# Attention values multiplied with tokens on partitions, and the convolution's first tap on GpSimd

## The chip, the core and the metric

The kernel runs on one core of one Trainium2 chip. The metric is the device time of one execution in microseconds; lower is better. The engines of the core are TensorE (PE: matmuls, with its weight loads as PEld), VectorE (DVE), ScalarE (ACT), GpSimd (POOL) and SyncE (SP, which here issues the loads of weights). Matmuls write to PSUM, a small memory of banks that DVE and ACT then evacuate to SBUF, the memory with 128 partitions on which all engines work.

## What is computed

Two layers of a hybrid block over 512 tokens with 256 tokens of context, model width 1024, float32. Cut to what the change touches, a layer is:

```python
zin = norm(x) @ w_in + b_in            # columns: rx, k, v, rg, q, cv, cg, g
# convolution branch
z = cv * sigmoid(cg)
z = depthwise_conv(z, dw_w, dw_b, (15, 15))   # 31 taps per channel
y_c = silu(layernorm(z)) @ w_conv_o
# recurrent branch: from rx (with context) and rg -> y_r
# attention branch: q, k, v, 8 heads, two softmaxes a head; v has 128 columns a head
w = p[:, :, 0] - lam * p[:, :, 1]
o = einsum('bhqk,bkhe->bqhe', w, v)
y_a = rmsnorm(o) @ w_o
# merge: three gates
m = sigmoid(g0) * y_r + sigmoid(g1) * y_a + sigmoid(g2) * y_c
```

Behind the merge comes a SwiGLU feed-forward. The values `v` and the keys cover context and tokens, 768 rows; the first layer also carries the context's own rows through the branches, the second layer only the 512 tokens.

## The kernel before

Activations lie with channels on partitions and tokens along the row: `u` is 8 blocks of 128 channels. A float32 product is made of three passes on rounded halves: high weights times high and low activations, and low weights times high activations. So each weight block of 1024 x 128 (a *job*, `Job`) is loaded raw by SP into one of three buffers, cast to its high half `whi` on ACT (L528), and subtracted to its low half `wlo` on DVE (L533); two buffers hold each half, and a few jobs borrow tiles `a` or `u`. PE then runs `kstep` (L379) for each of 8 channel blocks into one of three `sq` tiles of PSUM, two banks each, with the weights stationary and 384 tokens (twice) or 512 tokens moving, and ACT or DVE evacuates the tile. A job of 768 tokens is 48 matmuls of 384 columns; one of 512 tokens is 24 matmuls of 512 columns.

The jobs run strictly in the order of a list (`Stream`). In the convolution stage, for each of 8 blocks of channels, the list has the convolution's value job and its gate job, and then some *fill* jobs, as the table `FILL` (L39) says: attention values (`value_job`, one a head) and merge gates (`gate_job`). Behind that stage come the first jobs of the recurrent branch (rx, rg), the convolution's output jobs, the rest of the recurrent jobs with fill jobs from `FILL_RNN` between them, the first query and key jobs, and the recurrent branch's output jobs, into which the attention heads are woven.

Around this list a planner (`Plan`) writes the whole program. It keeps a clock for PE, ACT and DVE, prices each step, takes slots of PSUM and SBUF tiles into account, and emits at each point the ready step of the best priority. The order on each engine is fixed by that when the program is built: each engine runs its instructions in that order and waits wherever an input is late. The subtraction of a coming job's weights has priority 0.5, the gate of block b 4.5 + b, its taps 6 + b.

A convolution block goes thus: ACT makes the tanh of the gate projection (L977), DVE multiplies (`gate`, L992), ACT does the first tap with the bias (`tap0`, L998, a scale and a bias per partition over 783 or 512 columns), DVE does 29 taps (L1004) and the last one (L1014). A value job is evacuated by ACT (L1323), turned by PE in six 128x128 transposes (L1328) so that tokens come to lie on partitions, copied out of PSUM by ACT (L1332) and stored to DRAM by GpSimd's queue (L1334), from where attention loads it again.

Of the kernel before, what the change touches and what calls it, by code (L numbers as in the profile page):

```python
# [38 lines left out]
FILL = [[3, 3, 3, 3, 3, 3, 3, 3, 0, 3], [0, 2, 2, 2, 3, 3, 3, 3, 4, 1]]  # L39
FILL_RNN = [[0, 0, 0, 1, 0, 0, 2, 0, 0], [0, 0, 0, 0, 1, 1, 1, 0, 4]]  # L40
# [122 lines left out]
class Job:  # L163


    def __init__(self, xs, w, r0, c0, segs, done, nk=NB, start=None, acq="", frees=""):
        self.xs, self.w, self.r0, self.c0, self.nk = xs, w, r0, c0, nk
        self.start, self.done, self.acq, self.frees = start, done, acq, frees
        self.parts = [EVEN if segs is SEG else [(s0, n, s0) for s0, n in segs]]
        self.each, self.own, self.when = False, "", None  # L170
# [17 lines left out]
def kernel(ctx: ExitStack, tc: tile.TileContext, x, c, ctxt, c_ctx, w_mod, b_mod, g_norm1, g_norm2,  # L188
# [63 lines left out]
    vsp = [dp.tile([P, TA], F32, tag=f"vsp{j}", name=f"vsp{j}") for j in range(NB)]  # L252
# [120 lines left out]

    def kstep(ps, x, hi, lo, k, nk, segs):
# [15 lines left out]
    def start():  # L390
# [20 lines left out]
        for g in range(NB // 2):  # L411
# [9 lines left out]
            if g == 0:  # L421
                first_w.extend(wload(w_in[0], 0, NB, o) for o in (O_CV, O_CG, O_V))
# [49 lines left out]
    class Stream:  # L472


        def __init__(self):
            self.jobs, self.order, self.at, self.ps = [], [], 0, {}
            self.raws, self.ws, self.next, self.prepared, self.places = {}, {}, None, 0, [(), ()]

# [21 lines left out]
        def load(self, i):  # L500
            if i < len(self.jobs):
                j, box = self.jobs[i], []
                d = plan.dma(0.2 * j.nk, lambda: box.append(wload(j.w, j.r0, j.nk, j.c0)))
                self.raws[i] = box[0], d
# [10 lines left out]
        def split(self, i, own, after):  # L515
            rt, dm = self.raws.pop(i)
            nk = self.jobs[i].nk
# [4 lines left out]
            def high():  # L522
                if own:
                    tiles.extend([(at if own == "a" else ut)() for _ in range(-(-nk // kt))] for _ in range(2))
                box.extend([t[:, k * P:(k + 1) * P] for t in part for k in range(kt)] for part in tiles)
# [14 lines left out]
        def head(self):  # L540
            if self.next is None and self.at < len(self.order):
# [3 lines left out]
                for a0, an, steps in j.xs.parts:  # L545
                    if any(a0 < s0 + n and s0 < a0 + an for s0, n, _ in j.parts[p]):
                        if len(steps) <= k:
                            return None
                        deps += (steps[k],)
# [9 lines left out]
                self.next = Step(PE, 3 * w / 2400.0 + 0.01, self.emit, deps, 9, "" if k or p else "sq " + j.acq,  # L559
# [3 lines left out]
        def emit(self):  # L563
# [385 lines left out]
    def layer(l, r, u, norm2_seen, after_layer):  # L949
# [24 lines left out]
        def cg_job(b):  # L974
            def done(ps, k):
# [31 lines left out]
                def last():  # L1007
# [4 lines left out]
                    for s0, n in segs:  # L1012
# [6 lines left out]
                e = step(DVE, TW + 0.1, gate, e, prio=4.5 + b, rel="t2")  # L1019
                e = step(ACT, act_time(W) + 0.14, tap0, e, prio=2, acq="t")  # L1020
                fir_done.append(chain(DVE, [(w, lambda k=k: tap(k)) for k in range(1, CK - 1)]
                                      + [(w, last, "a", "t2")], e, prio=6 + b))
# [294 lines left out]
        def value_job(hd):  # L1317
            def done(v, ks):
                box = []

                def evac():
                    box.extend([tt(), tt()])
# [12 lines left out]

                s = step(ACT, act_time(TA), evac, ks, prio=0, acq="t2", rel="sq")
                for i, (s0, n) in enumerate(SEG):
                    p = step(PE, n / P * 0.11, lambda s0=s0, n=n: turn(s0, n), s, prio=1, acq="small")
                    s = step(ACT, act_time(n), lambda i=i, s0=s0, n=n: out(i, s0, n), p, prio=2,
                             rel="small t2" if i else "small")  # L1340
            return Job(u, w_in[l], 0, O_V + hd * P, SEG, done)

        fill = []
        for b in range(NB):
            fill += [value_job(b), gate_job(2, b), gate_job(0, b)]
# [52 lines left out]
        def head_steps(hd):  # L1398
# [3 lines left out]
            def values():  # L1402
                box.extend([tt(), tt()])
                box.append(plan.dma(0.8, lambda: sy.dma_start(box[0][:, 0:TA], vsp[hd])))
# [253 lines left out]
        first = len(stream.order) + 8 * (len(jobs) + 2)  # L1658
# [167 lines left out]
```

## Time and profile before

| | us |
|---|---|
| median of 3 runs | 3008.56 (3007.41 to 3008.78) |
| the profiled execution | 3010.61 |
| its span in the profile | 3008.8 |
| PE busy | 2957.3 (98%) |
| DVE busy | 2041.5 (68%) |
| ACT busy | 1303.6 (43%) |
| POOL busy | 136.4 (5%) |

The mean granted clock of the tensor engine was 0.993 of full speed. Rows of a timeline give the start of a run of equal instructions, how long the run lasted, the engine, the line, what is written and read with its shape, and how many instructions the run has; in brackets stands the idle time ahead of it and what ended it. Matmuls overlap, so the distance of two starts is their price and not the duration of one.

### The profile page before, as it was taken

To read this page: it belongs to the slowest core of one execution; us is meant where nothing else is said; L and a number is where in the kernel's file an instruction comes from. 1 tells how busy PE (TensorE), PEld (TensorE's weight loads), DVE (VectorE), ACT (ScalarE), POOL (GpSimd) and SP (SyncE) were. 2 spreads that over 40 slices of the span, in tenths; PEclk is the share of its full clock that TensorE was granted. 3 is DMA by queue.
4 is the path that set the end of the run, shared out by engine and by line. 5 is a ranking of instruction groups with operands and counts; after the bars stand their busy time and mean duration, and the time that the engine had idled before them with its cause. 6 is when DMAs were issued, how large, how long until landed. Compare 5 with 4: busy or idle time off the path is not lost.

```text
span 3008.8 us, 42526 instructions
## 1 busy us (share of the span) xinstructions
PE 2957.3 (98%) x16945; PEld 2734.5 (91%) x16945; DVE 2041.5 (68%) x2918; ACT 1303.6 (43%) x2088; POOL 136.4 (5%) x308
## 2 busy tenths in 40 slices
PE   7999999999999999999999999999999999999999
PEld 6999999999999899999999998888988888888887
DVE  5998887998577754898222279988786786533334
ACT  5222255684366633321211252347784566332223
POOL 1000000000001101000000000000001010000000
PEclk9999999999999999999999999999999999999999
DMA  8222224434421334555222233334235323523332
GB/s 266 93 92 91 84 84 157 150 104 158 126 64 54 93 103 125 167 199 183 64 63 63 69 106 105 120 106 133 81 100 169 89 69 94 157 77 96 95 97 85
DMA packets 442871, 333.36 MB, mean 111 GB/s; under 512 B 24370, under 2 KB 397650, under 8 KB 442672
## 3 DMA queue, kind: packets, MB, share of 16 engines
q1 hardware_dynamic: 433328, 294.45, 32.1%
q0 software_dynamic: 9344, 36.19, 3.3%
q8 instruction: 133, 2.18, 0.3%
q14 instruction: 66, 0.54, 0.1%
HBM read 281.29 MB, written 40.89 MB: 107 GB/s over the span
## 4 chain that ended last, share of the span: by engine, by line
PE 91%; DVE 3%; ACT 3%; DMA 1%; issue 1%; SPq 0%; ACTq 0%; DVEq 0%
PE sq L379 81%; PE small L1471 3%; PE sq L1435 3%; PE small L1462 2%; PE sq L1173 1%; DVE wlo L533 0%; ACT t L1447 0%; PE small L1328 0%; DMA raw<-in_w_ffn_in_dram 0%; PE small L636 0%; DVE t L616 0%; DMA t<-t 0%; PE small L1539 0%; DVE t L1222 0%; PE small L862 0%
## 5 line engine op out<-in xcount | busy, mean ns | idle before, releaser
L379 PE MATMUL sq<-u,whi 128*128 128x384 f32 (+2 forms) x6624 | 1587.6, 350 | 11.3 <-ACT u L727 3.0
L379 PEld LDWEIGHTS sq<-u,whi 128*128 128x128 f32 x6624 | 1175.3, 188 | 92.4 <-issue 13.6
L379 PE MATMUL sq<-u,wlo 128*128 128x384 f32 (+2 forms) x3312 | 958.5, 347 | 1.0 <-DVE wlo L533 1.0
L379 PEld LDWEIGHTS sq<-u,wlo 128*128 128x128 f32 x3312 | 607.3, 188 | 34.1 <-DVE wlo L533 1.5
L528 ACT CAST whi<-raw 128x1024 fp32r<-128x1024 f32 (+1 forms) x348 | 360.6, 1037 | 611.2 <-PE sq L379 566.2
L533 DVE TENSOR_TENSOR wlo<-raw,whi 128x1024 fp32r<-128x1024 f32 (+1 forms) x348 | 420.5, 1209 | 254.2 <-ACT whi L528 250.5
L379 PE MATMUL sq<-a,whi 128*128 128x384 f32 (+2 forms) x2160 | 531.6, 353 | 5.7 <-ACT t L1311 3.3
L379 PEld LDWEIGHTS sq<-a,whi 128*128 128x128 f32 x2160 | 384.9, 189 | 37.6 <-issue 4.2
L1004 DVE SCALAR_TENSOR_TENSOR t<-t,par 128x783 f32<-128x783 f32 (+1 forms) x464 | 399.1, 891 | 8.0
L379 PE MATMUL sq<-a,wlo 128*128 128x384 f32 (+2 forms) x1080 | 323.4, 350 | 0.0
L379 PEld LDWEIGHTS sq<-a,wlo 128*128 128x128 f32 x1080 | 198.9, 189 | 13.7
L1569 DVE SCALAR_TENSOR_TENSOR t<-sq,mod,t 128x512 f32<-128x512 f32 (+1 forms) x102 | 62.3, 633 | 197.6 <-PE sq L379 191.5
L616 DVE SCALAR_TENSOR_TENSOR t<-t,sT 128x512 f32<-128x512 f32 (+1 forms) x224 | 185.4, 881 | 6.0 <-DMA t<-in_w_mod_dram 6.0
L1447 ACT ACTIVATE t<-sq,s 128x768 f32<-128x768 f32 (+1 forms) x160 | 130.5, 822 | 30.9 <-DVE s L1440 30.2
L1440 DVE TENSOR_REDUCE s<-sq 128x1 f32<-128x768 f32 (+1 forms) x160 | 128.9, 844 | 18.1 <-PE sq L1435 17.7
L1628 DVE TENSOR_TENSOR t<-sq,t 128x768 f32<-128x768 f32 (+1 forms) x44 | 36.3, 824 | 140.7 <-PE sq L379 128.4
L1617 ACT ACTIVATE t<-sq 128x768 f32<-128x768 f32 (+1 forms) x44 | 31.1, 707 | 219.2 <-PE sq L379 213.2
L1435 PE MATMUL sq<-t 64*128 64x384 f32 (+1 forms) x864 | 96.3, 350 | 0.9 <-ACT t L1447 0.8
L1267 DVE SCALAR_TENSOR_TENSOR t<-t,sq 128x768 f32<-128x768 f32 (+1 forms) x48 | 39.2, 819 | 84.0 <-PE sq L379 82.6
L1311 ACT ACTIVATE t<-sq,par 128x768 f32<-128x768 f32 (+1 forms) x48 | 38.2, 797 | 132.7 <-PE sq L379 132.5
L1435 PEld LDWEIGHTS sq<-t 64*128 64x128 f32 x864 | 71.9, 186 | 17.7 <-issue 9.5
L1471 PE MATMUL small<-t,a 128*128 128x128 f32 x600 | 77.1, 276 | 1.3 <-ACT a L1465 1.3
(235 smaller groups left out, 2635.5 us busy)
## 6 DMA issues: line engine op xcount, KB each, us to landing
raw<-in_w_in_dram SPq DMA_DIRECT2D x160, 512.0 KB, 3.8
raw<-in_w_ffn_in_dram SPq DMA_DIRECT2D x88, 512.0 KB, 4.0
t<-in_w_mod_dram SPq DMA_DIRECT2D x64, 384.0 KB, 5.3
t<-in_w_mod_dram SPq DMA_DIRECT2D x64, 256.0 KB, 4.3
raw<-in_w_ffn_out_dram SPq DMA_DIRECT2D x32, 512.0 KB, 4.0
thg<-t POOLq DMA_DIRECT2D x24, 384.0 KB, 2.6
t<-thg SPq DMA_DIRECT2D x24, 384.0 KB, 4.8
raw<-in_w_conv_o_dram SPq DMA_DIRECT2D x16, 512.0 KB, 4.2
```

The source lines that it names most:

```text
L379: pe.matmul(ps[:, at_:at_ + n], a[k], b[:, s0:s0 + n], start=(k == 0 and i == 0), stop=(k == nk - 1 and i == 2))
L528: act.copy(t[:, 0:w], rt[:, q * n:q * n + w])
L533: vec.tensor_sub(o[:, 0:w], rt[:, q * n:q * n + w], t[:, 0:w].bitcast(F32))
L616: vec.scalar_tensor_tensor(a[:, 0:W], tiles[i][:, 0:W], f, a[:, 0:W], op0=ALU.mult, op1=ALU.add)
L1004: vec.scalar_tensor_tensor(acc[:, 0:W], zp[:, k:k + W], r.p[:, i:i + 1], acc[:, 0:W], op0=ALU.mult, op1=ALU.add)
L1267: vec.scalar_tensor_tensor(g[:, 0:T], g[:, 0:T], 1.0, ps[:, 0:T], op0=ALU.add, op1=ALU.mult)
L1435: pe.matmul(both[m][:, at_:at_ + n], q[a][mr, qsl], k[b][mr, s0:s0 + n], start=(i == 0), stop=(i == 2))
L1440: vec.tensor_reduce(mx[:, m:m + 1], sps[m][:, k0:TA], axis=AX.X, op=ALU.max, negate=True)
L1447: act.activation(es[m][:, 0:kw], sps[m][:, k0:TA], AF.Exp, bias=mx[:, m:m + 1], accum_out=sm[:, m:m + 1])
L1462: pe.transpose(tps[:, i:i + P], es[0][:, g0 + i:g0 + i + P], ident)
L1471: pe.matmul(ops[0][:, 0:P], wt[0][:, i * P:(i + 1) * P], vbox[0][:, vb * P:(vb + 1) * P], start=(i == 0), stop=(i == nk - 1))
L1569: vec.scalar_tensor_tensor(hj[:, ss], ps[:, at_:at_ + n], r.mod[:, ga * 8 + j, v:v + 1], hj[:, ss], op0=ALU.mult, op1=ALU.add)
```

## The change

Values are no longer computed a head at a time. The 1024 value columns are cut into two chunks of 512 (four heads). A chunk is four *turned* jobs, each with two of the eight channel blocks: now the activations are stationary, 128 channels x 128 tokens, and 512 weight columns move. So the result has tokens on partitions at once. A turned job goes over 6 blocks of tokens with 2 channel blocks and 3 passes each, 36 matmuls of 512 columns. The four jobs of a chunk add up in the same PSUM: all three `sq` tiles are held from the first to the last of them. DVE then adds the bias (a row broadcast to all partitions, loaded by SP) in six adds of 128x512, and GpSimd's queue stores each. The transposes and the evacuations and copies on ACT are gone. The chunks stand at fixed places in the list, behind the fill jobs of convolution blocks 2 and 5; the tables of fill jobs now hold merge gates alone, and in the second layer one gate job moves from behind the first key job into the convolution stage.

The first tap goes from ACT to GpSimd as a tensor_scalar behind the gate multiplication, and the planner gives it 0.5 us and 6.3 ns a column before the second tap may be planned.

```diff
-FILL = [[3, 3, 3, 3, 3, 3, 3, 3, 0, 3], [0, 2, 2, 2, 3, 3, 3, 3, 4, 1]]
-FILL_RNN = [[0, 0, 0, 1, 0, 0, 2, 0, 0], [0, 0, 0, 0, 1, 1, 1, 0, 4]]
+FILL = [[2, 3, 0, 3, 2, 0, 3, 3, 0, 3], [0, 2, 0, 2, 2, 0, 2, 3, 4, 1]]
+FILL_RNN = [[0, 0, 0, 1, 0, 0, 2, 0, 0], [0, 0, 0, 0, 1, 1, 1, 0, 3]]
+VALUES_AT = {2: 0, 5: 1}
...
+    def tstep(ps, xs, hi, lo, tb, q):
+        ss = slice(tb * P, (tb + 1) * P)
+        for k in range(2):
+            xh, xl = xs[2 * q + k]
+            for i, (a, b) in enumerate(((xh, hi), (xh, lo), (xl, hi))):
+                pe.matmul(ps, a[:, ss], b[k], start=(q == k == i == 0), stop=(q == 3 and k == 1 and i == 2))
...
+            if j.turned is not None:
+                if j.turned == 0 and k % 2 == 0:
+                    self.banks.append(sq())
+                ps = self.banks[k // 2][:, k % 2 * VC:(k % 2 + 1) * VC]
+                tstep(ps, j.xs, *self.ws[i][0], k, j.turned)
+                if j.turned == 3:
+                    j.done(ps, s, k)
...
-                def tap0():
                     acc = tt()
                     box.append(acc)
-                    act.activation(acc[:, 0:W], box[0][:, 0:W], AF.Identity, bias=r.p[:, PDB + b:PDB + b + 1],
-                                   scale=r.p[:, PDW + b:PDW + b + 1])
+                    gp.tensor_scalar(acc[:, 0:W], zp[:, 0:W], r.p[:, PDW + b:PDW + b + 1],
+                                     r.p[:, PDB + b:PDB + b + 1], op0=ALU.mult, op1=ALU.add)
+                    first.end = plan.now + TW + 0.1 + 0.4 + 0.0063 * W
...
-                e = step(DVE, TW + 0.1, gate, e, prio=4.5 + b, rel="t2")
-                e = step(ACT, act_time(W) + 0.14, tap0, e, prio=2, acq="t")
+                first = Step()
+                step(DVE, TW + 0.1, gate, e, prio=4.5 + b, acq="t", rel="t2")
...
-                    act.activation(box[0][:, 0:TA], v[:, 0:TA], AF.Identity, bias=pb(O_V, hd), scale=1.0)
-                def turn(s0, n):
-                    vt = small()
-                    for i in range(0, n, P):
-                        pe.transpose(vt[:, i:i + P], box[0][:, s0 + i:s0 + i + P], ident)
-                    box.append(vt)
-                def out(i, s0, n):
-                    act.copy(box[1][:, s0:s0 + n], box[2 + i][:, 0:n])
-                    if i == 1:
-                        gp.dma_start(vsp[hd], box[1][:, 0:TA])
...
+                def evac():
+                    o = tt()
+                    vec.tensor_add(o[:, 0:VC], ps, bt[:, 0:VC])
+                    gp.dma_start(vsp[c][:, :, tb * P:(tb + 1) * P], o[:, 0:VC].rearrange("p (h e) -> p h e", e=P))
...
             jobs += [cv_job(b), cg_job(b)] + fill_jobs(FILL[l][b])
+            jobs += value_jobs(VALUES_AT[b]) if b in VALUES_AT else []
```

In the changed kernel `tstep` is L399, `kstep` L406, the subtraction L566, the gate L1047, the first tap L1051, the taps L1058 and L1068, the values' add and store L1384 and L1385.

On PE, in layer 0, a value job stood before with its transposes woven into the job behind it (`sq` is the PSUM tile, `u` the activations, `a` and `whi` high or low weights):

```order
L379 MATMUL sq<-u,wlo 128x384 x2
L379 MATMUL sq<-u,a 128x384 x18
L1328 MATMUL small<-ident,t 128x128 x4
L379 MATMUL sq<-u,a 128x384 x12
L1328 MATMUL small<-ident,t 128x128 x2
L379 MATMUL sq<-u,a 128x384 x24
```

Now the first turned job of a chunk follows directly on a gate job:

```order
L406 MATMUL sq<-u,whi 128x384 x4
L406 MATMUL sq<-u,wlo 128x384 x2
L399 MATMUL sq<-whi,u 128x512
L399 MATMUL sq<-wlo,u 128x512
L399 MATMUL sq<-whi,u 128x512 x2
L399 MATMUL sq<-wlo,u 128x512
```

The transposes are gone, the weights are the moving operand, and the second matmul of a turned job reads the low half of the weights. The four jobs of a chunk stand one behind the other, with nothing between them.

On DVE, in layer 1's convolution stage, the taps (`t<-t,par`) and the subtractions (`wlo<-raw,whi`) stood before like this, from the first long run of taps on:

```order
L1004 SCALAR_TENSOR_TENSOR t<-t,par_11637 128x512 x12
L533 TENSOR_TENSOR wlo<-raw,whi 128x1024
L1004 SCALAR_TENSOR_TENSOR t<-t,par_11637 128x512 x7
L533 TENSOR_TENSOR wlo<-raw,whi 128x1024
L1004 SCALAR_TENSOR_TENSOR t<-t,par_11637 128x512 x6
...
L1004 SCALAR_TENSOR_TENSOR t<-t,par_11637 128x512 x12
L533 TENSOR_TENSOR wlo<-raw,whi 128x1024
L1004 SCALAR_TENSOR_TENSOR t<-t,par_11637 128x512 x6
L1014 SCALAR_TENSOR_TENSOR a<-t,par_11637 128x512
```

Now, from the fourth of these subtractions on (the ones for the first and the second turned job are the third and the fourth; the next one is that for the third turned job):

```order
L566 TENSOR_TENSOR wlo<-raw,whi 128x1024
L1058 SCALAR_TENSOR_TENSOR t<-t,par_11461 128x512 x24
L1068 SCALAR_TENSOR_TENSOR a<-t,par_11461 128x512
L1058 SCALAR_TENSOR_TENSOR t<-t,par_11461 128x512 x3
L1047 SCALAR_TENSOR_TENSOR t<-t 128x512
L1058 SCALAR_TENSOR_TENSOR t<-t,par_11461 128x512 x4
L1068 SCALAR_TENSOR_TENSOR a<-t,par_11461 128x512
L1058 SCALAR_TENSOR_TENSOR t<-t,par_11461 128x512 x2
L566 TENSOR_TENSOR wlo<-raw,whi 128x1024
L1058 SCALAR_TENSOR_TENSOR t<-t,par_11461 128x512 x9
```

Ahead of the first of the rows just shown, the long run of taps is cut by subtractions as before: one tap and a gate, 8 taps, a subtraction, 6 taps, a subtraction, 5 taps, a subtraction, 7 taps. Then 33 taps, two last taps and a gate stand between two subtractions.

On POOL, in layer 0's convolution stage, its memsets (of the padding around a convolution block) and stores stood before like this:

```order
L1313 DMA thg_0_107<-t 128x768
L986 MEMSET t 128x15
L987 MEMSET t 128x15
L989 MEMSET t 128x15
L1334 DMA vsp_132<-t 128x768
L1313 DMA thg_1_124<-t 128x768
```

Now the first tap stands behind each block's memsets, and a chunk's six stores stand together:

```order
L1044 MEMSET t 128x15
L1051 TENSOR_SCALAR t<-t,par_419 128x783
L1385 DMA vsp_131<-t 512x1x128 x6
L1041 MEMSET t 128x15
L1042 MEMSET t 128x15
L1044 MEMSET t 128x15
L1051 TENSOR_SCALAR t<-t,par_419 128x783
```

A first tap that waits for its gate now also holds up the stores behind it in this queue, and the other way round.

## Rows read from the trace of the kernel before

**Rows 1.** The page: PE's busy time; the chain that ended last, by engine.

```profile
PE 2957.3 (98%) x16945; PEld 2734.5 (91%) x16945; DVE 2041.5 (68%) x2918; ACT 1303.6 (43%) x2088; POOL 136.4 (5%) x308
...
PE 91%; DVE 3%; ACT 3%; DMA 1%; issue 1%; SPq 0%; ACTq 0%; DVEq 0%
```

**Rows 2.** Timeline of PE, layer 0's convolution stage: start, duration, line, shapes, count.

```profile
305.39 0.51 PE L379 MATMUL sq<-u,wlo 128*128 128x384 f32 x2
...
313.71 0.51 PE L379 MATMUL sq<-u,wlo 128*128 128x384 f32 x2
```

**Rows 3.** Timeline of PE, start of layer 1's convolution stage.

```profile
1790.42 0.87 PE L379 MATMUL sq<-u,whi 128*128 128x384 f32 x4
...
1800.86 0.60 PE L1328 MATMUL small<-ident,t 128*128 128x128 f32 x4
1801.22 0.71 PE L379 MATMUL sq<-u,whi 128*128 128x512 f32 x2
1801.77 0.39 PE L379 MATMUL sq<-u,wlo 128*128 128x512 f32 x1
...
1806.33 0.61 PE L379 MATMUL sq<-u,whi 128*128 128x512 f32 x2
...
1807.01 0.61 PE L379 MATMUL sq<-u,whi 128*128 128x512 f32 x2
```

**Rows 4.** Waits of PE, 1790 to 2014 us: total, times, longest.

```profile
PE small L1328 <- ACT t L1323: 2.0, 2, 1.0
PE sq L379 <- ACT t L1311: 1.6, 2, 0.8
PE sq L379 <- ACT t L969: 1.5, 1, 1.5
```

**Rows 5.** Busy time by stage: stretch, length, each engine's busy time, clock, DMA.

```profile
100.00:300.00 200.00, 200.00 (x1165) 199.66 (x1164) 184.10 (x188) 54.24 (x63) 9.13 (x30) 1.00 0.28 91
...
540.00:704.00 164.00, 161.42 (x935) 156.48 (x934) 161.30 (x221) 123.87 (x150) 2.91 (x15) 1.00 0.39 120
...
1800.00:2000.00 200.00, 194.96 (x945) 167.34 (x944) 193.70 (x265) 63.80 (x83) 11.69 (x32) 1.00 0.36 112
```

**Rows 6.** Groups by line and shape: an add of PSUM and SBUF on DVE.

```profile
L1628 DVE TENSOR_TENSOR t<-sq,t 128x512 f32<-128x512 f32 x22 | 15.2, 692 | 63.0 <-PE sq L379 55.0 <-ACT t L1617 8.0
```

**Rows 7.** Timeline of DVE, start of layer 1's convolution stage.

```profile
1792.40 0.69 DVE L992 SCALAR_TENSOR_TENSOR t<-t 128x512 f32<-128x512 f32 x1 [0.56 <-ACT t L977]
1793.01 0.42 DVE L914 TENSOR_TENSOR u<-t,u 128x256 fp32r<-128x256 f32 x1
1793.42 8.09 DVE L1004 SCALAR_TENSOR_TENSOR t<-t,par 128x512 f32<-128x512 f32 x12
1801.42 1.22 DVE L533 TENSOR_TENSOR wlo<-raw,whi 128x1024 fp32r<-128x1024 f32 x1
1802.56 4.72 DVE L1004 SCALAR_TENSOR_TENSOR t<-t,par 128x512 f32<-128x512 f32 x7
```

**Rows 8.** Timelines of DVE and PE at layer 1's first recurrent output job.

```profile
2271.18 0.69 DVE L938 TENSOR_TENSOR a<-t,a 128x512 fp32r<-128x512 f32 x1 [0.74 <-ACT a L932]
...
2274.44 0.61 PE L379 MATMUL sq<-a,whi 128*128 128x512 f32 x2
```

**Rows 9.** Timelines of POOL and DVE in the attention stage.

```profile
866.63 1.68 POOL L1523 TENSOR_SCALAR t<-t,s 128x128 f32<-128x128 f32 x1 [66.59 <-DVE s L1520]
...
937.02 3.12 POOL L1523 TENSOR_SCALAR t<-t,s 128x128 f32<-128x128 f32 x5
...
938.30 0.79 DVE L1369 TENSOR_TENSOR t<-t 128x512 f32<-128x512 f32 x1
...
983.98 0.69 DVE L1369 TENSOR_TENSOR t<-t 128x512 f32<-128x512 f32 x1
```

**Rows 10.** Timelines of DVE and PE at layer 1's first convolution output job.

```profile
2047.94 0.68 DVE L938 TENSOR_TENSOR a<-t,a 128x512 fp32r<-128x512 f32 x1
...
2062.61 0.62 PE L379 MATMUL sq<-a,whi 128*128 128x512 f32 x2
```

More of the change, by code (lines that the diff above doesn't have):

```diff
@@ L169, in __init__, with turned_job @@
         self.parts = [EVEN if segs is SEG else [(s0, n, s0) for s0, n in segs]]
-        self.each, self.own, self.when = False, "", None
+        self.each, self.own, self.when, self.turned = False, "", None, None
+VC = 4 * P
+def turned_job(xs, w, c0, q, done, start=None, acq=""):
+    j = Job(xs, w, 2 * q * P, c0, [(0, TA)], done, nk=TA // P, start=start, acq=acq)
+    j.turned = q
+    return j
 HALVES = [(0, S // 2, 0), (S // 2, S // 2, S)]
@@ L251 @@
     thg = [[dp.tile([P, TA], F32, tag=f"thg{r}_{j}", name=f"thg{r}_{j}") for j in range(NB)] for r in range(3)]
[L252 removed]
+    vsp = [dp.tile([P, 4, TA], F32, tag=f"vsp{j}", name=f"vsp{j}") for j in range(2)]
     part = [dp.tile([P, TA], F32, tag=f"part{j}", name=f"part{j}") for j in range(NB)]
@@ L516, in split @@
             rt, dm = self.raws.pop(i)
-            nk = self.jobs[i].nk
+            turned = self.jobs[i].turned is not None
+            nk = NB if turned else self.jobs[i].nk
             kt, tiles = (4, []) if own else (nk, [[wp.tile([P, 1024], F32R, tag=tag, name=tag)] for tag in ("whi", "wlo")])
@@ L524, in high @@
                     tiles.extend([(at if own == "a" else ut)() for _ in range(-(-nk // kt))] for _ in range(2))
-                box.extend([t[:, k * P:(k + 1) * P] for t in part for k in range(kt)] for part in tiles)
+                w = VC if turned else P
+                box.extend([t[:, k:k + w] for t in part for k in range(0, kt * P, w)] for part in tiles)
                 for q, t in enumerate(tiles[0]):
@@ L558, in head @@
                 last = final and k == j.nk - 1
-                self.next = Step(PE, 3 * w / 2400.0 + 0.01, self.emit, deps, 9, "" if k or p else "sq " + j.acq,
+                acq = "" if k or p else j.acq
+                if j.turned is None:
+                    acq += "" if k or p else " sq"
+                else:
+                    w = 2 * VC
+                    acq += " sq" if j.turned == 0 and k % 2 == 0 else ""
+                self.next = Step(PE, 3 * w / 2400.0 + 0.01, self.emit, deps, 9, acq,
                                  (j.frees if final else "") + (f" {j.own}4" if j.own and last else ""), j.when)
@@ L1315, in gate_job, with value_jobs, start, done @@
             return Job(u, w_in[l], 0, O_G + br * D + b * P, segs, done)
[L1317 to L1341 removed]
+        def value_jobs(c):
+            bias, outs_ = [], []
+            def start():
+                t = tt()
+                bias.append((t, plan.dma(0.8, lambda: sy.dma_start(t[:, 0:VC], b_in[l:l + 1, c0:c0 + VC].to_broadcast([P, VC])))))
+            def done(ps, ks, tb):
+                (bt, d), = bias
+                def evac():
+                    o = tt()
+                    vec.tensor_add(o[:, 0:VC], ps, bt[:, 0:VC])
+                    gp.dma_start(vsp[c][:, :, tb * P:(tb + 1) * P], o[:, 0:VC].rearrange("p (h e) -> p h e", e=P))
+                outs_.append(step(DVE, vec_time(VC), evac, ks, d, *outs_[-1:], prio=0, acq="t",
+                                  rel="t" + (" sq" if tb % 2 else "") + (" t" if tb == TA // P - 1 else "")))
+            c0 = O_V + c * VC
+            return [turned_job(u, w_in[l], c0, q, done, start=None if q else start, acq="" if q else "t") for q in range(4)]
         fill = []
         for b in range(NB):
[L1345 removed]
+            fill += [gate_job(2, b), gate_job(0, b)]
         fill += [gate_job(1, b) for b in range(NB)]
@@ L1657, in layer @@
         jobs += [q_job(0), k_job(0)] + fill_jobs(FILL_RNN[l][NB])
-        first = len(stream.order) + 8 * (len(jobs) + 2)
+        first = len(stream.order) + 8 * (len(jobs) + 2) - 2 * 8
         for j in jobs[1:4:2] if l else jobs[2:4]:
```

32 lines of the change are left out of this document (25 added, 7 removed).

## The prediction

> **What bounds the kernel now.** I read the page first: the tensor engine (PE) is busy 98% of the span and carries 91% of the chain that ended last [rows 1]. So a matmul taken away is time won, unless PE then waits for something it does not wait for now. The timelines give PE's price list. In layer 0 the two rows lie 8.32 us apart, with 48 matmuls of 384 columns between them: 173 ns each [rows 2]. In layer 1 three matmuls of 512 columns take 0.68 us: 227 ns each [rows 3]. The same group shows what a value job costs beside its products: four transposes push the next matmul 0.36 us on, and the two behind take 0.55 us instead of 2 x 0.227, 0.10 more; together 0.46 us. Half of that, 0.23, is taken for the two others of a job: 0.69 us. Then I read the waits of PE in layer 1's convolution stage: 2.0 us there are transposes waiting for the value's evacuation, 3.1 us are matmuls waiting for other evacuations [rows 4]. Last, the busy time by stage, to see which engine stands right behind PE. The vector engine (DVE) is busy 184 of 200 us in layer 0's convolution stage, 161.3 of 164 us before the recurrent branch's output jobs, and 193.7 of 200 us in layer 1's convolution stage [rows 5]. PE leads, but in three stages DVE has next to no room. That decides this case.
>
> **The change part by part.**
>
> *Products of the values.* Per layer, 8 jobs of 48 matmuls at 173 ns (66.6 us) become 8 jobs of 36 at 227 ns (65.3 us): -1.3 us [rows 2, 3].
>
> *Transposes.* 48 per layer go: 8 x 0.69 = -5.5 us. Their waits go too, -2.0 us in layer 1 [rows 4]; for layer 0 I count none. On PE alone this makes -6.8 us in layer 0 and -8.8 us in layer 1, all of it on PE's path. The 48 evacuations and copies that leave ScalarE (ACT) I count at nothing: ACT is not what PE waits for, outside the waits just named.
>
> *Twelve adds a layer on DVE.* A 128x512 add that reads PSUM takes 692 ns [rows 6]; back to back, instructions of this size start some 0.61 us apart (the 512-column gate does so [rows 7]), so 7.3 us a layer land on an engine that is nearly full. In layer 0 the stage has 16 us idle in 200 [rows 5], some 26 over its 330 us, which hides them if the idle time lies where they are needed: 0 to +4 us, taken +2.
>
> *Order of DVE in layer 1.* This is the largest term. PE's second matmul of a job needs the low half of its weights, which DVE makes. The order of before brings such a subtraction every 5 to 12 taps; after the change one stretch has 33 taps, two last taps and a gate between the subtraction for the second job of the first value chunk and that for its third. When does each engine get there? PE: the job behind the first gate projection starts at 1790.42 [rows 3]. By the new order two gate jobs (24 x 227 ns = 5.44 us each), the next two convolution jobs (as long) and two value jobs (36 x 227 ns = 8.16 us) stand before the third: 1790.42 + 21.8 + 16.3 = 1828.5. DVE: its first long run of taps starts at 1793.42 [rows 7]; one tap more now stands before it, so 1794.1. Twelve taps take 8.09 us, the last of them 0.75, so taps are 0.667 us apart; a subtraction takes 1.14 us from its start to the next tap's start; a gate 0.61. Up to the subtraction in question stand 61 taps (40.7 us), 4 subtractions (4.6) and one gate (0.6): it starts at 1840.0 and ends at 1841.2. So PE waits 1841.2 - 1828.7 = **12.5 us**, once, in layer 1. Nothing hides it: PE takes its jobs strictly in turn, and DVE is full there. If the tap on GpSimd slows DVE, it becomes 14. In layer 0, and for layer 1's second chunk, the order has a subtraction every 5 to 10 taps, and no such gap.
>
> A wait of that length lets evacuations catch up, so the 3.1 us of other waits [rows 4] may vanish: 0 to -3.1, taken -1.5.
>
> *One gate job moved* from behind the last key job into layer 1's convolution stage. It costs 5.4 us early and gives them back late, if the late place is on PE's path. There the last split of the recurrent branch, which hangs on a gate product ahead of the moved job, ends at 2271.9, and PE starts on the last eighth of the first output job, which needs it, at 2274.4 [rows 8]. PE can come only 2.6 us earlier before it waits: +2.8 net, bounds 0 and +2.8.
>
> *Layer 0's recurrent stage* ends with the same kind of split, and DVE is busy 161.3 of 164 us before it [rows 5], so what DVE has more to do comes late at PE. Priced instruction by instruction at mean durations, DVE has 168.9 us of work between the last convolution-output job and that split before, and 170.7 after, since some instructions are placed otherwise: +1.8 us.
>
> *The first tap on GpSimd.* The trace has no such pass. The nearest row is a scaling of 128x128: five in 3.12 us, 0.62 us each [rows 9]. By elements, a pass of 783 takes 3.8 us and one of 512 takes 2.5 us; from below the fixed part bounds them, 0.62. A gain is excluded on DVE, which does its 30 taps as before. GpSimd itself is idle. What counts is how the two engines get in each other's way. While that scaling ran, a DVE add took 0.79 us; the same line without it took 0.69 [rows 9]: 0.10 us, by elements 0.6 us for a pass of 783 and 0.4 for 512. Over 8 passes a layer that is 4.9 and 3.2 us of DVE time. I take it as hidden in layer 0's idle time and inside the 12.5 to 14 us in layer 1. The other way round, one scaling took 1.68 us, with DVE adds of two SBUF inputs running back to back beside it [rows 9]: GpSimd waits for DVE. The taps are instructions of that kind too, which is a rival below.
>
> The Trainium skill ("SBUF — State Buffer", section "Who interferes with whom") states that a DVE instruction with two SBUF inputs contends with a GpSimd instruction that reads SBUF, and that the shared ports are an exclusive lock. The trace agrees that GpSimd is held back, but DVE lost 0.10 us to a pass of 0.62 [rows 9], far from all of it. By the rule DVE would lose the whole pass (rival 3); by the row, a sixth of it.
>
> **The sum.** Layer 0: -6.8 + 1.8 + 2 = -3.0 (from -5.0 to -1.0). Layer 1: -8.8 + 12.5 - 1.5 + 2.8 = +5.0 (from +0.6 to +8.0). Together +2.0, from -4.4 to +7.0. The profiled execution took 3010.61 us, 2.05 above the median of the runs: 3012.6 there, **3010.6** as a median, from 3004 to 3018. Most of what PE wins it waits away.
>
> **The rivals.**
>
> 1. *PE keeps its whole saving*: -6.8 - 8.8 = -15.6, so 3008.6 - 15.6 = **2993**. For it: PE is 91% of the chain [rows 1], and no other engine leads for long. Against it: DVE would have to reach one subtraction 12 us sooner than its taps allow. What could make it so is that tensor time lost in the convolution stage is won back behind it, in stages where PE waits at present.
>
> 2. *GpSimd gets in only when DVE stops*: slower. In a run of taps back to back the pass finds no gap; DVE then comes to the first tap of that block, waits, and pays the pass alone: 2.5 us x 8 = 20 us in layer 1. Of this the slack behind the stage takes a part. The last split of the convolution's result ends at 2048.6, and PE needs it 21 matmuls (4.8 us) after 2062.61 [rows 10]: 18.8 us, less 7.3 for the adds, is 11.5. So it decides from 11.5 / 8 = 1.4 us a pass, and at 2.5 costs 8.5 us: 3010.6 + 8.5 = **3019**. For it: the scaling of 1.68 us. Against it: that one did get in, and the plan leaves each pass some microseconds while DVE works on another block. In layer 0 the same costs 8 x 3.8 = 30 us against 26 idle, which adds up to some 10 more: 3029.
>
> 3. *GpSimd holds DVE for its whole pass, and first waits out a tap*: 2.5 + 0.75 us, 8 times in layer 1, is 26 us, less 11.5: +14.5. In layer 0 it is 8 x (3.8 + 1.0) = 38 us against 26 less the adds' 7.3: +20 at most, taken as half. 3010.6 + 24.5 = **3035**. This is what the exclusive lock would do. Against it: the 0.10 us of [rows 9].
>
> **How the numbers follow.** Forecast 0.45, rival 1 0.25, rival 2 0.21, rival 3 0.07, something unnamed 0.02. About 0.2%, 6 us, is what a measurement of this kernel can tell from no change: 3002.5 to 3014.6 is the same. Of the forecast 0.07 falls below that (if layer 1's wait is partly won back), 0.06 above, 0.32 inside; of rival 2 0.03 is inside and 0.18 above. Faster 0.25 + 0.07 + 0.01 = 0.33; same 0.35; slower 0.06 + 0.18 + 0.07 + 0.01 = 0.32. Cases of both signs hold over half, so beside the likeliest's own range (3004 to 3018) stands the range for 8 in 10: 2993 to 3026, which leaves out the lower half of rival 1 and most of rival 3.
>
> **What would show it.** Right: one wait of PE of 12 to 14 us on the low half of the weights, at the third value job in layer 1, and none like it in layer 0; no transposes in the value stage; PE busy some 16 us less; a wait of up to 3 us for the last split in layer 1. GpSimd's first taps should take 2.5 to 5 us, with DVE waiting for them for less than 3 us in a layer. Wrong: if that one wait is missing or short (rival 1); if DVE waits for GpSimd eight times for over 1.4 us (rival 2); if taps beside a pass take as long as the pass (rival 3).

## The result: slower by half a per cent

| | median us | range | ratio to before, 95% interval |
|---|---|---|---|
| before | 3008.11 | 3007.41 to 3008.78 (4 runs) | |
| changed | 3023.43 | 3020.53 to 3026.29 (4 runs) | 1.0055 [1.0043, 1.0066] |
| changed, once more | 3021.79 | 3020.66 to 3029.31 (5 runs) | 1.0062 [1.0048, 1.0075] |

The profiled execution took 3020.91 us, its span is 3019.1. The change costs about 15 us. The forecast of 3010.6 was 11 to 13 us too low. Its own range, 3004 to 3018, did not hold the result; the wide range for 8 in 10, 2993 to 3026, did, and that one left both signs open. By the 6 us that the prediction takes for what can be told from no change, this is slower, where it took the same for likeliest.

The page of the changed kernel (busy time, share, instructions; below it the chain that ended last), to be read against [rows 1]:

```profile
PE 2946.3 (98%) x16657; PEld 2700.5 (89%) x16657; DVE 2065.7 (68%) x2942; ACT 1257.8 (42%) x2023; POOL 179.0 (6%) x332
...
PE 87%; DVE 6%; ACT 4%; DMA 2%; issue 1%; SPq 0%; ACTq 0%; DVEq 0%
```

PE is busy 11 us less (16 was forecast; matmuls at a lower clock count as busy for longer), and still ends later. Its share of the chain fell from 91% to 87%, and DVE's rose from 3% to 6%: PE now waits more. For whom, the waits of PE over the whole span say (total, times, longest):

```profile
PE sq L399 <- DVE wlo L566: 13.8, 1, 13.8
PE sq L1227 <- ACT t L1194: 8.0, 8, 2.7
PE small L1511 <- DVE t L1502: 5.2, 2, 4.8
PE sq L1227 <- ACT t L1232: 4.4, 4, 1.8
```

The first row is the wait that the prediction named: one, at the low half of the weights of the third value job. In the timeline of DVE in layer 1 the 24 taps in a row can be seen, and the subtraction that comes behind them:

```profile
1814.28 1.23 DVE L566 TENSOR_TENSOR wlo<-raw,whi 128x1024 fp32r<-128x1024 f32 x1
1815.42 15.99 DVE L1058 SCALAR_TENSOR_TENSOR t<-t,par 128x512 f32<-128x512 f32 x24
...
1840.48 1.22 DVE L566 TENSOR_TENSOR wlo<-raw,whi 128x1024 fp32r<-128x1024 f32 x1
1841.62 7.05 DVE L1058 SCALAR_TENSOR_TENSOR t<-t,par 128x512 f32<-128x512 f32 x9
```

The timeline of PE at the same place:

```profile
1827.32 0.62 PE L399 MATMUL sq<-whi,u 128*128 128x512 f32 x2
1841.76 0.80 PE L399 MATMUL sq<-wlo,u 128*128 128x512 f32 x1 [13.83 <-DVE wlo L566]
1842.35 1.05 PE L399 MATMUL sq<-whi,u 128*128 128x512 f32 x2
1843.20 0.63 PE L399 MATMUL sq<-wlo,u 128*128 128x512 f32 x1
...
1844.90 0.63 PE L399 MATMUL sq<-whi,u 128*128 128x512 f32 x2
```

Behind the wait the starts are 0.43 us apart instead of 0.23: two matmuls from 1842.35 take 0.85 us, where three took 0.68 in [rows 3]. The windows (stretch, length, busy times, granted clock, DMA) say why:

```profile
1842.00:1843.00 1.00, 1.00 (x3) 0.81 (x4) 0.96 (x2) 0.00 (x0) 0.00 (x0) 0.50 0.13 27
1848.00:1850.00 2.00, 2.00 (x11) 1.65 (x10) 2.00 (x3) 0.00 (x0) 0.00 (x0) 1.00 0.00 0
```

The granted clock was 0.50, the lower of its two levels (1.2 of 2.4 GHz), after PE had stood still, and 1.00 further on. The seven intervals from 1841.76 to 1844.90 take 3.14 us instead of 1.59, so the wait costs 1.55 us beyond itself.

**Where the time went**, by the distance between the same DVE and ACT instructions in the two traces (medians over stretches of 100 us): the changed kernel is 3.3 us ahead at 300 to 400 us and 3.0 ahead behind layer 0's recurrent stage, still 1.7 ahead at 1700, then some 15 behind at 1900 to 2000 (there the two orders differ, and the figure is rough), 11.4 behind at 2100, 12.6 behind at 2300 to 2400 and 10.6 behind at the end. So layer 1's mixing stages cost some 14 us, and layer 0 gave some 3, of which 1.7 was left at its end. This compares two executions, of which one kernel's differ by some us among themselves.

**Layer 0's recurrent gates.** The second row of the waits lies mostly in layer 0. The waits of PE from 400 to 760 us, of the changed kernel:

```profile
PE sq L1227 <- ACT t L1194: 7.8, 7, 2.7
PE sq L1227 <- ACT t L1232: 2.3, 2, 1.8
PE sq L1227 <- DVE t L1102: 2.1, 1, 2.1
```

and of the kernel before:

```profile
PE sq L1173 <- ACT t L1140: 3.2, 4, 1.2
PE sq L379 <- DVE a L938: 1.9, 1, 1.9
PE sq L379 <- ACT t L1178: 1.4, 2, 1.1
```

L1227 (L1173 before) is the product of a recurrent gate; L1194, L1232 and L1102 read PSUM tiles that it needs. It is a handful of matmuls, and in the timeline of the changed kernel they start at 429.83 us, where before the first of them starts at 448.37:

```profile
429.83 0.86 PE L1227 MATMUL sq<-t,gwh 128*128 128x384 f32 x4
...
433.70 0.98 PE L1227 MATMUL sq<-t,gwh 128*128 128x384 f32 x4 [2.65 <-ACT t L1194]
...
437.14 1.65 PE L1227 MATMUL sq<-t,gwh 128*128 128x384 f32 x4 [2.12 <-DVE t L1102]
```

They stand so early in PE's order that their PSUM tiles are not free: PE waits for evacuations. From 435 to 446 us the granted clock is 0.53, and the last row's four matmuls take 1.65 us instead of 0.86.

**GpSimd's pass.** Groups by line and shape:

```profile
L1051 POOL TENSOR_SCALAR t<-t,par 128x783 f32<-128x783 f32 x8 | 19.6, 2453 | 112.1 <-issue 61.5 <-DVE t L1047 50.6
L1051 POOL TENSOR_SCALAR t<-t,par 128x512 f32<-128x512 f32 x8 | 14.4, 1799 | 96.6 <-issue 85.9 <-DVE t L1047 10.8
L1058 DVE SCALAR_TENSOR_TENSOR t<-t,par 128x783 f32<-128x783 f32 x232 | 240.3, 1047 | 5.2
L1058 DVE SCALAR_TENSOR_TENSOR t<-t,par 128x512 f32<-128x512 f32 x232 | 168.5, 760 | 4.0 <-POOL t L1051 0.6
L1384 DVE TENSOR_TENSOR t<-sq,t 128x512 f32<-128x512 f32 x24 | 16.5, 686 | 2.2 <-PE sq L399 2.0
```

It takes 2.45 us for 783 columns and 1.80 for 512. DVE waited for it 0.6 us in the whole program. The taps' means are 1047 and 760 ns; before they were 1033 and 748.

Most of a pass is waiting. The timelines of POOL and DVE, for the first pass, which met a DVE with little to do, and for the second:

```profile
68.46 1.01 POOL L1051 TENSOR_SCALAR t<-t,par 128x783 f32<-128x783 f32 x1
...
92.63 2.70 POOL L1051 TENSOR_SCALAR t<-t,par 128x783 f32<-128x783 f32 x1 [15.49 <-issue]
...
93.50 1.03 DVE L1058 SCALAR_TENSOR_TENSOR t<-t,par 128x783 f32<-128x783 f32 x1
94.56 1.59 DVE L1058 SCALAR_TENSOR_TENSOR t<-t,par 128x783 f32<-128x783 f32 x1
```

The second pass ends 0.81 us after the first tap's end, and the tap that begins in between takes 1.59 us instead of 1.03. The other passes look alike: each ends 0.72 to 0.81 us (783 columns) or 0.48 to 0.64 us (512) after the end of a tap or a subtraction on DVE, and nearly always the DVE instruction behind that is 0.31 to 0.57 us longer than its kind.

### The profile page after: what moved, and what is told of

It is laid out like the page before. It is cut to its first block, busy times and chain, and to the rows that moved or that the text cites. A ratio compares the mean times of both kernels' runs of the same rounds, so it can differ in the third digit from the quotient of the medians.

```text
span 3019.1 us, 41940 instructions
## 1 busy us (share of the span) xinstructions
PE 2946.3 (98%) x16657; PEld 2700.5 (89%) x16657; DVE 2065.7 (68%) x2942; ACT 1257.8 (42%) x2023; POOL 179.0 (6%) x332
## 4 chain that ended last, share of the span: by engine, by line
PE 87%; DVE 6%; ACT 4%; DMA 2%; issue 1%; SPq 0%; ACTq 0%; DVEq 0%
PE sq L406 73%; PE sq L399 4%; PE small L1520 3%; PE sq L1484 3%; PE small L1511 1%; PE sq L1227 1%; DVE t L1058 1%; DVE wlo L566 1%; ACT t L1496 1%; DMA raw<-in_w_in_dram 0%; DMA raw<-in_w_ffn_in_dram 0%; ACT whi L561 0%; DVE t L671 0%; DMA t<-in_w_mod_dram 0%; DVE t L1276 0%
## 5 line engine op out<-in xcount | busy, mean ns | idle before, releaser
L406 PE MATMUL sq<-u,whi 128*128 128x384 f32 (+2 forms) x6112 | 1476.6, 351 | 6.2 <-ACT u L782 3.6
L406 PEld LDWEIGHTS sq<-u,whi 128*128 128x128 f32 x6112 | 1087.6, 189 | 86.9 <-issue 13.8
L406 PE MATMUL sq<-u,wlo 128*128 128x384 f32 (+2 forms) x3056 | 894.0, 348 | 1.0 <-DVE wlo L566 1.0
L406 PEld LDWEIGHTS sq<-u,wlo 128*128 128x128 f32 x3056 | 561.1, 188 | 34.0 <-DVE wlo L566 1.9
L566 DVE TENSOR_TENSOR wlo<-raw,whi 128x1024 fp32r<-128x1024 f32 (+1 forms) x348 | 421.3, 1211 | 248.0 <-ACT whi L561 244.3
L406 PE MATMUL sq<-a,whi 128*128 128x384 f32 (+2 forms) x2160 | 531.6, 353 | 6.2 <-ACT t L1365 3.3
L406 PEld LDWEIGHTS sq<-a,whi 128*128 128x128 f32 x2160 | 384.3, 189 | 39.0 <-ACT t L1365 4.0
L1058 DVE SCALAR_TENSOR_TENSOR t<-t,par 128x783 f32<-128x783 f32 (+1 forms) x464 | 408.8, 904 | 9.3 <-POOL t L1051 0.6
L406 PE MATMUL sq<-a,wlo 128*128 128x384 f32 (+2 forms) x1080 | 323.2, 350 | 0.0
L406 PEld LDWEIGHTS sq<-a,wlo 128*128 128x128 f32 x1080 | 198.5, 188 | 13.6
L399 PE MATMUL sq<-whi,u 128*128 128x512 f32 x384 | 119.9, 392 | 0.0
L399 PE MATMUL sq<-wlo,u 128*128 128x512 f32 x192 | 75.7, 394 | 13.8 <-DVE wlo L566 13.8
```

The source lines that it names most:

```text
L399: pe.matmul(ps, a[:, ss], b[k], start=(q == k == i == 0), stop=(q == 3 and k == 1 and i == 2))
L406: pe.matmul(ps[:, at_:at_ + n], a[k], b[:, s0:s0 + n], start=(k == 0 and i == 0), stop=(k == nk - 1 and i == 2))
L566: vec.tensor_sub(o[:, 0:w], rt[:, q * n:q * n + w], t[:, 0:w].bitcast(F32))
L1058: vec.scalar_tensor_tensor(acc[:, 0:W], zp[:, k:k + W], r.p[:, i:i + 1], acc[:, 0:W], op0=ALU.mult, op1=ALU.add)
```

## The experiments

Each group of runs has runs of the kernel before on the same chip beside it; their median was 3006.5 to 3007.4. Ratios are to those.

### Is the one wait what costs, and must it be?

The cause of the long run of taps lies in the plan. The evacuation of a convolution value block waits, in the plan, for the last tap of the block two before it. In layer 1 the third block's evacuation therefore waits for the first block's 31 taps, and holds a PSUM tile that the first value chunk needs; so the plan lets DVE go on with taps. On the chip PE had no wait for that tile: in this stage it waits once, for the low half. The first run takes that tie away for this block:

```diff
-conv_out[b] = step(ACT, TT, f, k, *fir_done[b - 2:b - 1] if b > 1 else (), prio=0, acq="t3",
+conv_out[b] = step(ACT, TT, f, k, *(fir_done[b - 2:b - 1] if b > (1 if co else 2) else ()), prio=0, acq="t3",
```

> The changed kernel with one edit: in the plan of layer 1, the evacuation of the third convolution value job no longer waits for the first block's last tap. The list of jobs stays; on the vector engine the subtraction for the third value job of the first chunk moves ahead of about 24 taps. Theory A (the one wait of 13.8 us and the 1.6 us of half-speed matmuls behind it are what the change costs in layer 1, and behind them the stage has room for half of it): 3023.4 - 8 = 3015, from 3010 to 3018, with no wait of PE over 3 us in the convolution stage. Theory B (PE is what counts there): all 15.4 us come back, 3008. Theory C (the vector engine bounds the stage, which must do its taps anyway): the wait moves behind the last tap, 3019 to 3024.

Measured: 3013.26 us, 1.0019 [1.0010, 1.0028]. The waits of PE in layer 1's convolution stage (1790 to 2030 us) are now

```profile
PE sq L399 <- DVE wlo L566: 1.7, 1, 1.7
PE sq L406 <- ACT t L1365: 0.8, 1, 0.8
PE sq L406 <- DVE wlo L566: 0.6, 1, 0.6
```

and DVE is busy 197.4 of the 200 us from 1800 on. Of the 15.4 us that the wait and the slow matmuls cost, 8.5 to 10 came back: theory A. That the rest is the full DVE fits this number, but no run shows it by itself.

The second run moves the chunks:

```diff
-FILL = [..., [0, 2, 0, 2, 2, 0, 2, 3, 4, 1]]
+FILL = [..., [0, 0, 2, 2, 0, 2, 2, 3, 4, 1]]
-VALUES_AT = {2: 0, 5: 1}
+VALUES_AT = [{2: 0, 5: 1}, {1: 0, 4: 1}]
```

> The changed kernel with layer 1's two value chunks behind convolution blocks 1 and 4 instead of 2 and 5, and its fill jobs placed as 0, 0, 2, 2, 0, 2, 2, 3, 4, 1. No stretch of more than 14 us of taps stands between two subtractions there. Theory A (the placement of the chunk behind a long run of taps makes the wait, not the turned values as such): no wait over 3 us, 3010 to 3017. Theory B (a chunk holds all three PSUM tiles, so wherever it stands something waits as long): 3020 or more.

Measured: 3012.49 us, 1.0019 [1.0009, 1.0028]; the longest wait there is 1.8 us. Holding all three PSUM tiles is not what makes the wait. It is where the chunk stands against the taps.

The changed kernel was run beside later ones, unchanged:

> The changed kernel once more, beside the others of this group, since its executions lay in two groups (3020.5 and 3026): 3023 within 3 us, and the wait of 13.8 us at the third value job of layer 1 again.

Measured: 3021.79 us, with the wait of 13.8 us.

### Does the tap belong on GpSimd?

Put back to ScalarE, with the values still turned:

```diff
-gp.tensor_scalar(acc[:, 0:W], zp[:, 0:W], r.p[:, PDW + b:PDW + b + 1],
-                 r.p[:, PDB + b:PDB + b + 1], op0=ALU.mult, op1=ALU.add)
-first.end = plan.now + TW + 0.1 + 0.4 + 0.0063 * W
+act.activation(acc[:, 0:W], box[0][:, 0:W], AF.Identity, bias=r.p[:, PDB + b:PDB + b + 1],
+               scale=r.p[:, PDW + b:PDW + b + 1])
```

> The changed kernel with the first tap on ScalarE again, as before the change; the values stay turned. Theory A (GpSimd's pass costs the vector engine next to nothing: 0.6 us of waiting in the whole program): the wait at the third value job stays at 12 to 17 us, since the long run of taps is still there, and the time stays at 3023 within 4 us. Theory B (the pass slows the taps or comes late): 3015 or less.

Measured: 3012.9 us, 1.0016 [1.0007, 1.0025]. Neither theory as written: the wait stayed (11.7 + 4.1 us, the first part on the cast and the second on the subtraction) and yet the time fell by 9 to 10 us. So the tap on GpSimd, with the order that the plan makes of it, cost something that is not DVE's waiting for GpSimd. Alone, on the kernel before, it cost too:

> The kernel before with the first tap on GpSimd alone; values as before. Theory A: no change within 3 us of before (3008), from 3005 to 3011, since ScalarE is not what anyone waits for at that place. Theory B (GpSimd's pass holds the vector engine or is held up by it): 3012 or more.

Measured: 3014.32 us, 1.0020 [1.0012, 1.0029]: theory B by its number. But DVE does not stand out in the trace; the waits of PE (400 to 760 us) do, and they are those of the changed kernel:

```profile
PE sq L1172 <- ACT t L1139: 5.6, 5, 2.7
PE sq L1172 <- ACT t L1177: 2.3, 2, 1.8
PE sq L1172 <- DVE t L1047: 1.5, 1, 1.5
```

That points at the order. The plan prices the pass at 0.4 us and 6.3 ns a column beside the gate, 5.3 us in all for 783 columns, where it took 2.48 in that run. While the plan's DVE has no tap ready it can take other steps earlier, and PE, with them, the recurrent gates. The next run tests this by changing one number:

```diff
-first.end = plan.now + TW + 0.1 + 0.4 + 0.0063 * W
+first.end = plan.now + TW + 0.1 + 0.4 + 0.0026 * W
```

> The kernel before with the first tap on GpSimd, as in the run of that name, but with the pass priced in the plan at 0.4 us and 2.6 ns a column, which is what it took there (2.48 us for 783 columns), instead of 0.4 us and 6.3 ns. The work is the same; only the order differs, and layer 0's first recurrent gate products stand 20 rows later on PE. Theory A (the price, which pulled those products ahead of their inputs, makes the run with the tap alone slower: 3014.3 against 3007.4): 3007 to 3010. Theory B (the pass itself does): 3013 or more.

Measured: 3000.91 us, 0.9982 [0.9974, 0.9991], 13 us less than with the other price and 6 less than before, below theory A's own bounds. All that is left of PE's waits from 400 to 760 us:

```profile
PE sq L1172 <- ACT t L1139: 1.3, 2, 0.7
PE sq L379 <- ACT t L1177: 0.9, 1, 0.9
PE small L646 <- DVE t L1474: 0.4, 1, 0.4
```

Is that a gain of GpSimd or of the order? The next run keeps this kernel's order on PE and DVE word for word and issues the tap on ScalarE at the same place:

```diff
-gp.tensor_scalar(acc[:, 0:W], zp[:, 0:W], r.p[:, PDW + b:PDW + b + 1],
-                 r.p[:, PDB + b:PDB + b + 1], op0=ALU.mult, op1=ALU.add)
+act.activation(acc[:, 0:W], zp[:, 0:W], AF.Identity, bias=r.p[:, PDB + b:PDB + b + 1],
+               scale=r.p[:, PDW + b:PDW + b + 1])
```

> The kernel of the run with the tap alone and repriced (3000.9), with its order word for word on PE and the vector engine, but the first tap issued on ScalarE at the same place. So the order of that run is kept and the engine is the old one. Theory A (the order is what gained: the recurrent gates and the last split of layer 0 come in time): 2999 to 3003. Theory B (taking the tap off ScalarE is what gained): 3005 to 3009, with waits of PE on ScalarE in layer 0's convolution stage or at its recurrent gates.

Measured: 3000.65 us, 0.9980 [0.9971, 0.9989]. The same as on GpSimd: in this order the engine of the first tap is worth nothing that can be told, and the order alone is worth -6 us. At the other price the kernel is 7 us slower than before; the same order with the tap on ScalarE was not run, so that all of the 7 is the order's is argued from the 13 us that the price alone moves.

### Do the two costs add up, and what are turned values worth?

Both repairs, each repair alone, and the values alone:

> The changed kernel with the subtraction early (3013.3) and the pass priced as measured. Theory A (in layer 0 PE waits 7.8 us for the recurrent gates' evacuations and runs some 10 us at half speed behind, for the price alone): 3004 to 3009, with less than 4 us of that wait. Theory B (these waits come from the turned values): 3012 to 3015.

> The changed kernel with nothing but the pass repriced; the long run of taps stays. Theory A (the two costs add up: repricing alone takes away some 11 to 14 us of the 3022, the early subtraction the other 10): 3008 to 3012, with the wait of 13 to 15 us at the third value job. Theory B (they are one and the same cost): 3000 or 3020.

> The turned values alone: the changed kernel with the first tap on ScalarE as before, and with the subtraction early. Against 3012.9 with the tap on ScalarE and the long wait still in. Theory A (half to all of the 15.8 us waited there comes back): 2998 to 3005, faster than before. Theory B (the stage is bound by the vector engine, so the wait moves): 3009 or more.

| subtraction early | pass repriced | median us | ratio |
|---|---|---|---|
| no | no | 3021.79 to 3023.43 | 1.0055 to 1.0062 |
| yes | no | 3013.26 | 1.0019 [1.0010, 1.0028] |
| no | yes | 3007.96 | 1.0007 [0.9998, 1.0016] |
| yes | yes | 2999.48 | 0.9976 [0.9967, 0.9986] |
| yes | tap on ScalarE | 3004.43 | 0.9991 [0.9983, 1.0000] |

The early subtraction is worth 8.5 to 10 us and the price 14 to 15.5; together they took 22 to 24. They add up. Traced by distances as above, the price alone moves layer 0 from 3.0 us ahead to 8.9 (behind its recurrent stage), and layer 1's mixing stages from 14 us lost to 8. So in the changed kernel less than half of what the price is worth lies in layer 0; with the tap alone most of it does (1.9 behind, then 9.5 ahead). The run with the price alone still has its wait:

```profile
PE sq L399 <- DVE wlo L566: 13.2, 1, 13.2
```

It came out 0.04 us below what theory A gave, and the values alone inside theirs, though hardly faster than before: their interval ends at 1.0000. Both repairs together came out 4.5 us below theory A; of the gates' wait on L1194, 1.3 us are left. Turned values in layer 0 alone, with the tap repriced:

> Turned values in layer 0 alone, layer 1's values and fill jobs as before the change; the tap on GpSimd repriced in both. Against the tap alone, repriced (3000.9). Theory A (layer 0 keeps its 6.8 us of tensor time, less what its vector engine needs more): 2996 to 2999, since layer 1's full vector engine gains nothing from turning. Theory B (turning is worth nothing in layer 0 either): 3000 to 3002.

Measured: 3000.31 us, 0.9979 [0.9969, 0.9989], against 3000.91 without any turned values: theory B. Of the 6.8 us that PE has less to do in layer 0, nothing is left that can be told in the time. From 400 to 760 us PE waits for ScalarE's evacuations of the recurrent gates and for a split instead:

```profile
PE sq L406 <- ACT t L1232: 2.1, 2, 1.1
PE sq L1227 <- ACT t L1232: 2.0, 1, 2.0
PE sq L1227 <- ACT t L1194: 1.3, 2, 0.7
PE sq L406 <- DVE a L993: 1.0, 1, 1.0
```

### The moved gate job

In the changed kernel PE waits 4.8 us at layer 1's first recurrent output job. Its timeline:

```profile
2272.08 0.73 PE L406 MATMUL sq<-a,whi 128*128 128x512 f32 x2
...
2285.42 1.51 PE L1511 MATMUL small<-ident,t 128*128 128x128 f32 x6 [4.78 <-DVE t L1502]
2286.59 1.20 PE L406 MATMUL sq<-a,whi 128*128 128x512 f32 x2
```

and DVE's:

```profile
2278.22 1.99 DVE L1276 TENSOR_TENSOR_SCAN t<-t 128x256 f32<-128x256 f32 x2
...
2284.26 1.02 DVE L1502 SCALAR_TENSOR_TENSOR t<-t,s 128x768 f32<-128x768 f32 x1
2285.19 0.68 DVE L993 TENSOR_TENSOR a<-t,a 128x512 fp32r<-128x512 f32 x1
```

PE waits for L1502, a head's combination of its two softmaxes, for six transposes. In DVE's order that stands behind the last scan (L1276) and just ahead of the last split (L993). The matmuls behind run at half speed once more (granted clock 0.50 from 2286 to 2287). Both repairs leave this wait as it was, 4.8 us. With the gate job put back, on top of them:

```diff
-FILL = [..., [0, 2, 0, 2, 2, 0, 2, 3, 4, 1]]
-FILL_RNN = [..., [0, 0, 0, 0, 1, 1, 1, 0, 3]]
+FILL = [..., [0, 2, 0, 2, 2, 0, 2, 2, 4, 1]]
+FILL_RNN = [..., [0, 0, 0, 0, 1, 1, 1, 0, 4]]
```

> As the changed kernel with the subtraction early and the pass repriced (2999.5), and with layer 1's moved gate job back behind the first key job. PE's work is the same. Theory A (the wait of 4.8 us of a head's transposes at the first recurrent output job, and the matmuls at half speed behind it, are there because PE comes 5.4 us earlier than the vector engine's chain): that wait shrinks to under 1 us and the time falls by 3 to 6, to 2994 to 2997. Theory B (the chain itself is late, so the wait follows it): 2998 to 3001.

Measured: 2995.63 us, 0.9961 [0.9949, 0.9974]. The wait is gone; from 2240 to 2290 us PE waits for nothing but

```profile
PE sq L406 <- ACT t L1496: 0.5, 1, 0.5
```

Theory A, though 3.9 us is not far above what two kernels here can be told apart by. This is the fastest version here, 11.6 us below the kernel before.

## Why the prediction was half right

**The one wait: right.** It was forecast at 12.5 us with the subtraction ending at 1841.2; it was 13.8, with the subtraction running from 1840.48 and PE going on at 1841.76. PE came there 0.8 us earlier than reckoned. Some luck is in it: DVE began its stretch 1.2 us earlier than reckoned and took 48.9 us for it instead of 47.1, with two of GpSimd's passes beside its taps. The other waits of the stage vanished altogether (between 1790 and 2030 us PE has this wait and no other), 1.6 us more than the step took.

**What a wait costs behind itself: left out.** Each long wait was followed by matmuls at the lower granted clock: 1.55 us behind the 13.8, some 1.5 behind the 4.8 (four intervals of 1.85 us in all instead of 0.91, and before them six transposes of 1.17 us instead of 0.57), and a longer stretch at layer 0's gates. No term of the sum had that, though the kernel before shows a lower clock too: 0.84 from 425 to 435 us.

**The price of the tap: right on the chip, wrong in the plan.** The bounds for the pass (0.62 to 3.8 and 2.5 us) held, 2.45 and 1.80; the sign that it would take 2.5 to 5 us did not. The taps became 14 and 12 ns longer, over 232 taps 3.2 and 2.8 us, against 4.9 and 3.2 forecast. DVE's wait of 0.6 us throws out rival 2; that its 3019 lies nearest to the result is chance. Rival 3 is out as it was priced: DVE lost some 6 us, where the rival had 26 and 38. Its mechanism is not out. The ends of the passes and the longer instructions beside them fit two engines that shut each other out; the rival took the whole pass for the time that DVE is held, and most of a pass is GpSimd's own waiting.

What the step left out is the plan. It took the new order as given and looked for its gaps on DVE alone. What the plan's price did to PE's order in layer 0 (the first recurrent gates stand 14 rows of the timeline behind the norm's first statistics, where before it was 44, and ahead of free PSUM tiles) stands in no term. The runs show the size of what was left out: repricing alone is worth 14 us in the changed kernel, some 6 of it in layer 0, and 13 in the one with the tap alone.

**Layer 0: right by luck.** It was forecast at -3.0 and stood 3.0 us ahead behind its recurrent stage. But with the price repaired it stands 8.9 ahead there, and with the tap on ScalarE 8.7. So the order cost some 6 us that no term had, and the rest of the sum was too dear by as much. Which term is not traced. The tap alone, repriced, stands 9.5 ahead without any turned value, so that gain need not come from turning; the terms of 1.8 and 2 us for DVE were not tested by any run.

**Slack behind layer 1's convolution: wrong.** Rival 2's working put 11.5 us between the last split and PE's need, after the adds. There was none. The last tap ended at 2022.5 us (2003.8 before). The adds were counted, at 7.3 us. What was not counted is in the taps: from start to next start, the 232 taps of layer 1 take 171.9 us instead of 164.9. The taps beside a pass account for some 2.8 us. In the row of 24 taps above they start 0.66 us apart, in the row of 9 from 1841.62 on 0.79; of the longer distance there are 97, where before there were 32. With the subtraction early there are 66 and the sum is 165.4; with the tap on ScalarE there are still 82. So this comes with the order, whichever engine does the first tap. Likely the longer distance is that of a tap behind one of its own block, whose result it reads; the trace does not show blocks. With that, the first convolution output job waits 0.7 us for a cast and 0.2 for a split at 2075, and a recurrent gate 1.8 us at 2086, at the lower clock behind it.

**The moved gate job: right in kind, mis-sized.** The step was that PE comes early and waits for the recurrent chain, +2.8 net. The wait fell on a head's transposes, which hang on an instruction that DVE's order has put behind that chain's scan, and it was 4.8 us, some 6.3 with the slow matmuls behind. Taking the wait from the split alone, and not from all that stands ahead of it in DVE's order, is what failed.

**The sum.** The part of layer 1 was forecast at +5.0 and is some +14. The windows of layer 1's mixing stages, before and changed:

```profile
1764.00:2330.00 566.00, 558.00 (x2849) 489.16 (x2848) 469.20 (x639) 320.38 (x445) 30.64 (x91) 1.00 0.38 116
...
1764.00:2330.00 566.00, 542.28 (x2642) 464.58 (x2643) 476.43 (x642) 297.14 (x407) 47.88 (x100) 0.98 0.37 112
```

PE stands idle 23.7 us instead of 8.0, 15.7 more, where the sum's waits came to 13.8 (12.5 - 1.5 + 2.8). So the waits explain 2 of the 9 us missed. If PE's work shrank by the 8.8 us of the forecast, the other 7 are matmuls at the lower clock, 0.98 in the mean instead of 1.00: about 1.5 each are seen behind the 13.8 and the 4.8, and some 2.5 between 2073 and 2091; the rest is not traced to a row. On this reckoning the largest miss is the term that was not there, the clock behind a wait.

**Rival 1** (the tensor saving lands whole) is out for the change as it stands. With the repairs, the best version gains 11.6 us, but the order that came with the tap alone gave 6 in a kernel without turned values.

## What to carry to other kernels

Where a planner sets the order, a new price or a new tie in the plan moves work on engines that the change does not touch: compare the order on the bottleneck engine at every stage, above all where a product moved ahead of its inputs. A move to another engine is tested by keeping the order and changing the engine alone; here that showed that the engine was worth nothing, while one price in the plan moved 13 us. And a saving on the leading engine is worth what the second engine leaves: where that one is busy 97%, a change of its order can take the gain back, as the layer 1 here shows.

## What the runs showed of the hardware

The executions of one kernel differ by up to some 10 us, and the time goes with the mean granted clock of the execution. The kernel with the chunks moved took 3008.18 us at a mean of 0.992 and 3018.76 at 0.988; the kernel before took 3003.97 at 0.996 and 3010.25 at 0.994. In the three stretches named above (435 to 446, 1842 to 1843 and 2286 to 2287 us; 0.53, 0.50 and 0.50) the clock is at or near its lower level right behind or among waits of PE. So a wait should be priced with a tail; and with intervals of some 3 us to either side, a difference of under 3 us between two kernels is not told apart here.

GpSimd did get in beside taps that run back to back, but only once one of them had ended. The pass over 512 columns took 1.31 us in one place (from 1792.84 us) and 2.19 in another, and both ended 0.56 us after a tap's end; at its end a pass cost DVE 0.31 to 0.57 us. This is read from the records of 16 passes in one trace; no run was made to test it.
